# Rows split into half-precision parts and transposed by DMA, and half-precision pairs for queries and keys

## Chip, cores and metric

The kernel runs on one core of one Trainium2 chip. The metric is the device time of one execution in microseconds; the median of three runs is given. All times below come from the runs, from one profiled execution or from its trace.

## The reference

One layer of a hybrid encoder on 2048 rows of width 1024, all in float32:

- `h = rmsnorm(x)`, then one projection `h @ w_in` gives the queries, keys and values of 4 stick-breaking heads and of 8 chunked heads, and three 256-wide inputs of a gated convolution of width 3.
- Stick-breaking heads: `A[t,s] = sigmoid(z_ts) * prod over s<j<t of (1 - sigmoid(z_tj))`, with `z = q.k / 8` and `s < t`; the output is `A @ v`.
- Chunked heads: queries and keys are RMS-normalised per head (width 64), each chunk of 64 rows attends to itself and the 8 chunks before it, with a relative-position bias and a softmax.
- All outputs are RMS-normalised per head (`y`), then `x = x + y @ w_out`.
- `x = x + (silu(g @ w_gate) * (g @ w_up)) @ w_down`, with `g = rmsnorm(x)`; the inner width is 2816.

## The kernel before

Products run on TensorE as three matmuls of half-precision pairs: a float32 operand is split into a high part and the rest, and high x high, high x low and low x high are added in PSUM (`mm3`, lines 315 to 321). Both operands need the contracted dimension on the partitions, so every 128 normalised rows have to be transposed first.

The 2048 rows are cut in two halves of two groups of 512 rows. `hh` and `hl` are the transposed high and low parts of a group; there is one buffer of each for either group of a half, and the x rows, the y rows (normalised outputs of the heads) and the rows of the feed-forward all use them in turn. A class `Rows` (lines 341 to 371) makes them two blocks of 128 rows at a time: `ahead` calls `make` (load and normalise, `rms_rows`) and `to_T`, `need` makes sure that a pair is there, and `beside` spreads the next pair over the matmuls of the present one. `to_T` (lines 265 to 277) transposes 8 times on TensorE into a PSUM buffer of the tag `sc`, which the scores use too; ScalarE then copies the high part out and VectorE subtracts it to make the low part.

The program has four parts. `weave` interleaves by hand two generators: `fill` makes projections, convolutions, the normalisation of y and the first half's output projection, and `attend` gives pieces of attention. A clock of written-out costs (the numbers that the generators yield) says when the next piece of attention is taken; TensorE keeps this order. Attention pieces run in three steps, with a lag of 3 and 5 pieces between them: scores and weights (`front`), transposes of the weights (`mid`), product with V (`back`). Then come `ffn(0)`, the output projection of the second half (`out_proj`), and `ffn(1)`. The other engines' order is made by a scheduler. All transfers are issued by SyncE's queue (SP), in order: weights, rows, Q, K and V, stores of attention outputs and of intermediate results in DRAM. GpSimd subtracts for the low parts of weights (line 225) and adds the two halves of each finished attention tile (`put_y`, line 574).

Queries and keys go to DRAM (`kd`, `qd`) as high and low parts in F32R, written by `put_parts` (lines 423 to 431), and come back in `attend`: K holds the high part on 64 partitions and the low part on the other 64, and two query tiles hold the two orders, so that two matmuls give all products (`scores`, lines 577 to 587). For a piece of one key block (n = 1) `scores` also computes the 128 columns ahead of it. `y_norm` (lines 706 to 720) normalises y and stores it to `ynd`, from which `y_rows` loads it.

Of the kernel before, what the change touches and what calls it, by code (L numbers as in the profile page):

```python
# [22 lines left out]
NEG = -1e30  # L23
WSC = float(2 ** 14)
# [15 lines left out]
def trunk(ctx: ExitStack, tc: tile.TileContext, x, anw, w_in, qnw, knw, biasx, conv_w, onw, w_out,  # L40
# [18 lines left out]
    xp = ctx.enter_context(tc.tile_pool(name="xp", bufs=6))  # L59
# [12 lines left out]
    nc.gpsimd.affine_select(out=never, in_=never, pattern=[[1, 128]], compare_op=ALU.is_gt, fill=NEG,  # L72
# [4 lines left out]
    cw = consts.tile([128, 2, 3], F32, name="cw")  # L77
    halo = consts.tile([128, 2, 2], F32, name="halo")
# [4 lines left out]
    ynd = [dp.tile([128, D], F32, name=f"ynd{t}") for t in range(NB)]  # L83
# [181 lines left out]
    def to_T(xn, hh, hl, t):  # L265

        cs = slice(t * 128, (t + 1) * 128)
        for i in range(2):
            p = sc1()
            ks = slice(4 * i, 4 * i + 4)  # L270
            for k in range(4):
                c = (4 * i + k) * 128
                nc.tensor.transpose(p[:, k * 128:(k + 1) * 128], xn[:, c:c + 128], ident)  # L273
            pk = p.rearrange("p (k c) -> p k c", k=4)
            nc.scalar.copy(hh[:, ks, cs], pk)
            nc.vector.tensor_tensor(hl[:, ks, cs], pk, hh[:, ks, cs], ALU.subtract)
            yield 0.45
# [46 lines left out]
    kd, qd = [{(p, i, j): dp.tile([128, HT], F32R, name=f"{n}d{p}_{i}{j}")  # L324
# [8 lines left out]
    def late_consts():  # L333
        for i, w in enumerate((qnw, knw)):
            for s in range(2):
                nc.sync.dma_start(nw[s * 64:(s + 1) * 64, i:i + 1], w.rearrange("(p o) -> p o", o=1))
        nc.vector.tensor_scalar(nw[:, 0:1], nw[:, 0:1], HD ** -0.5, None, op0=ALU.mult)
        for b in range(2):
            nc.sync.dma_start(cw[:, b, :], conv_w[:, b * 128:(b + 1) * 128].rearrange("t p -> p t"))
# [115 lines left out]
    def stick_qk(H, groups, W, pair):  # L455
        key = ("qk", pair)
        u = W.get(key)
        for i, d in enumerate((kd, qd)):
            yield from proj_T(H, groups, u[i], lambda g, o, i=i, d=d: put_parts(o, pair, g, d, descale(key, i)))
# [117 lines left out]
    def scores(Q, cols, K, k0, n, diagonal=False):  # L577
# [3 lines left out]
        lead = 128 if n == 128 else 0  # L581
        kc = K[:, k0 - lead:k0 + n]
        nc.tensor.matmul(z[:, :n + lead], q1[:, cols], kc, start=True, stop=False)  # L583
        if diagonal:
            nc.tensor.matmul(z[:, lead:lead + 128], identb, never, start=False, stop=False)
        nc.tensor.matmul(z[:, :n + lead], q2[:, cols], kc, start=False, stop=True)
        return z[:, lead:lead + n]
# [4 lines left out]
    def stick_tile(T, head, K, k0, Q, V, cols):  # L592
# [3 lines left out]
        def piece(b, n):  # L596
# [3 lines left out]
            def front():  # L600
# [4 lines left out]
                nc.scalar.activation(be[:, :N], z, AF.Sigmoid, scale=HD ** -0.5)  # L605
                nc.scalar.activation(re[:, :N], z, AF.Sigmoid, scale=-HD ** -0.5)  # L606
# [28 lines left out]
    def chunk_tile(T, head, K, k0, Q, V, cols, bias):  # L635
# [4 lines left out]
        def front():  # L640
# [9 lines left out]
            nc.vector.tensor_scalar(nm, m[:, 0:1], other, -1.0, op0=ALU.max, op1=ALU.mult)  # L650
            tot = small(1, "tot")
            nc.scalar.activation(s[:, :n * 128], s[:, :n * 128], AF.Exp, bias=nm, accum_out=tot)
# [15 lines left out]
    def attend(half, groups, head):  # L668
# [4 lines left out]
        K = ap.tile([128, HT + more], F32R, name="k", tag="k")  # L673
        V = ap.tile([128, (HT + more) // 128, 2, HD], F16, name="v", tag="v")
        rows = slice(head % 2 * 64, head % 2 * 64 + 64)
        for j in range(2):
            at = slice(j * 64, j * 64 + 64)
            nc.sync.dma_start(f32(K[at, :HT]), f32(kd[head // 2, half, j][rows, :]))
            if more:
                nc.sync.dma_start(f32(K[at, HT:]), f32(kd[head // 2, 0, j][rows, :more]))  # L680
# [3 lines left out]
        if not stick:  # L684
            bias = ap.tile([128, CW], F32, name="bias", tag="bias")
            nc.sync.dma_start(bias, biasx[head - 4])
            nc.gpsimd.memset(bias[0:64, 576:640], NEG)
            nc.gpsimd.memset(bias[64:128, 0:64], NEG)
        for g in groups:
            c = where(g)[1]  # L690
            q1 = ap.tile([128, GRP], F32R, name="q1", tag="q")
            q2 = ap.tile([128, GRP], F32R, name="q2", tag="q")
            for j in range(2):
                src = f32(qd[head // 2, half, j][rows, c:c + GRP])
                for i, q in enumerate((q1, q2)):
                    at = (i + j) % 2 * 64
                    nc.sync.dma_start(f32(q[at:at + 64, :]), src)
# [8 lines left out]
    def y_norm(T, gain, tmp):  # L706
# [13 lines left out]
        nc.sync.dma_start(ynd[T], yt)  # L720
# [30 lines left out]
    def ffn_rows(H, groups):  # L751
        gain = []

        def make(g, b):
# [4 lines left out]
            return rms_rows(xt, gain[0])  # L759
# [260 lines left out]
```

## Time and profile before

| what | value |
|---|---|
| runs | 2720.06 us median of 3 (2718.31 to 2722.84) |
| profiled execution | 2721.8 us |
| its span, first to last instruction | 2719.9 us |
| granted TensorE clock, mean | 0.978 |
| TensorE busy | 2548.8 us (94%) |
| VectorE, ScalarE, GpSimd busy | 1472.0, 1046.1, 358.3 us |
| moved by DMA | 327.82 MB, 120 GB/s of HBM traffic over the span |

The span is what the trace shows; the time of the execution has some 2 us around it. Busy shares are means over stages of different kinds, so the windows by stage have to be read with them: the interleaved part lasts to about 1190 us, `ffn(0)` to 1910, the second output projection to 2036, and `ffn(1)` to the end. A granted clock of 1 is 2.4 GHz, 0.5 is 1.2 GHz.

### The profile page before, as it was taken

What the parts mean: (1) busy time and instruction counts of PE and PEld (TensorE: products, weight loads), DVE (VectorE), ACT (ScalarE), POOL (GpSimd) and SP (SyncE); (2) the same over time, 40 slices, a digit from 0 to 9 for tenths busy, and PEclk for the clock granted to TensorE, in tenths of its full rate; (3) what the DMA queues carried; (4) which work ended last, traced back from release to release, by engine and by line L of the source; (5) the groups of instructions that cost most, each with busy time, mean ns of one, the idle gap of its engine ahead of it and who ended that gap; (6) DMA issues with size and microseconds to landing.
All of it is one profiled execution on the core that took longest, in us unless ns stands there. A gap on an engine that the chain in (4) does not pass through costs nothing.

```text
span 2719.9 us, 41796 instructions
## 1 busy us (share of the span) xinstructions
PE 2548.8 (94%) x16258; PEld 1719.7 (63%) x16258; DVE 1472.0 (54%) x3535; ACT 1046.1 (38%) x1994; POOL 358.3 (13%) x389
## 2 busy tenths in 40 slices
PE   5998979998799889879999999999999999999999
PEld 4477766766687578754555555556864555555556
DVE  6467777689999878853443444333352333322234
ACT  5565756555455677663333333321121111111110
POOL 1123331102212211021111111110000000000000
PEclk8999989999999999989999999999999999999999
DMA  7644546554332267664332223232661111111101
GB/s 246 192 139 131 164 140 201 171 167 134 128 120 72 88 177 200 200 223 141 101 101 93 93 93 101 78 101 104 229 210 47 47 47 47 59 58 47 47 24 62
DMA packets 245063, 327.82 MB, mean 121 GB/s; under 512 B 77184, under 2 KB 168320, under 8 KB 244864
## 3 DMA queue, kind: packets, MB, share of 16 engines
q1 hardware_dynamic: 244864, 325.14, 37.8%
q8 instruction: 128, 2.10, 0.3%
q14 instruction: 71, 0.58, 0.1%
HBM read 220.21 MB, written 104.86 MB: 120 GB/s over the span
## 4 chain that ended last, share of the span: by engine, by line
PE 38%; DMA 4%; issue 4%; DVE 2%; POOL 1%; ACT 1%; SPq 0%; POOLq 0%; DVEq 0%; ACTq 0%
PE acc L318 7%; PE acc L320 7%; PE acc L319 7%; PE sc L937 5%; PE sc L938 5%; PE sc L939 5%; POOL w L225 1%; DMA wr<-in_w_down 1%; DMA x1d<-xs 1%; DMA wr<-in_w_up 1%; PE sc L273 0%; DMA xf<-x1d 0%; DVE gl L923 0%; DVE x L941 0%; DVE wl L258 0%
## 5 line engine op out<-in xcount | busy, mean ns | idle before, releaser
L318 PE MATMUL acc<-hh,w 128*128 128x512 f16 x1728 | 657.5, 381 | 0.0
L319 PE MATMUL acc<-hl,w 128*128 128x512 f16 x1728 | 656.3, 380 | 0.0
L320 PE MATMUL acc<-hh,w 128*128 128x512 f16 x1728 | 656.1, 380 | 0.0
L919 DVE SCALAR_TENSOR_TENSOR sg<-acc,ds,sg 128x512 f32<-128x512 f32 x88 | 66.0, 750 | 615.3 <-PE acc L320 533.5
L318 PE MATMUL acc<-w,hh 128*128 128x256 f16 x1408 | 392.5, 279 | 5.5 <-ACT w L224 4.0
L319 PE MATMUL acc<-w,hh 128*128 128x256 f16 x1408 | 390.4, 277 | 1.8 <-POOL w L225 1.8
L320 PE MATMUL acc<-w,hl 128*128 128x256 f16 x1408 | 390.1, 277 | 1.3 <-DVE rry L102 1.3
L941 DVE TENSOR_TENSOR x<-sc,x 128x512 f32<-128x512 f32 x352 | 241.3, 690 | 200.5 <-PE sc L939 193.7
L320 PEld LDWEIGHTS <-w 128*128 128x128 f16 x1728 | 169.3, 98 | 204.9 <-issue 1.8
L318 PEld LDWEIGHTS <-w 128*128 128x128 f16 x1728 | 169.3, 98 | 192.3 <-issue 15.8
L937 PE MATMUL sc<-wh,gh 128*128 128x512 f32 x704 | 278.7, 396 | 4.5 <-DVE x L941 4.5
L319 PEld LDWEIGHTS <-w 128*128 128x128 f16 x1728 | 169.6, 98 | 175.1 <-issue 1.1
L939 PE MATMUL sc<-wh,gl 128*128 128x512 f32 x704 | 274.2, 390 | 0.0
L938 PE MATMUL sc<-wl,gh 128*128 128x512 f32 x704 | 274.2, 389 | 0.0
L225 POOL TENSOR_TENSOR w<-wr,w 128x1024 f16<-128x1024 f32 x76 | 163.4, 2170 | 579.1 <-ACT w L224 523.6
L551 DVE SCALAR_TENSOR_TENSOR wtl<-tp,wth 128x512 f16<-128x512 f32 (+3 forms) x384 | 200.0, 529 | 50.5 <-ACT wth L550 49.7
L609 DVE TENSOR_TENSOR_SCAN re<-re,zero 128x512 f32<-128x512 f32 (+3 forms) x160 | 185.8, 1161 | 48.6 <-ACT re L606 48.3
L550 ACT ACTIVATE wth<-tp 128x512 f16<-128x512 f32 (+3 forms) x384 | 175.5, 475 | 81.9 <-PE tp L548 79.0
L922 ACT CAST gh<-sg 128x512 fp32r<-128x512 f32 x88 | 54.3, 617 | 378.7 <-DVE sg L919 378.7
L583 PE MATMUL sc<-k,q 128*128 128x320 f32 (+3 forms) x384 | 161.8, 425 | 4.8 <-ACT re L606 1.8
L318 PEld LDWEIGHTS <-hh 128*128 128x128 f16 x1408 | 140.1, 100 | 41.1 <-issue 19.9
L223 ACT ACTIVATE wr<-wr,wsc 128x1024 f32<-128x1024 f32 x76 | 83.4, 1141 | 191.2 <-DVE wsc L214 191.1
(153 smaller groups left out, 3798.2 us busy)
## 6 DMA issues: line engine op xcount, KB each, us to landing
w<-wd SPq DMA_DIRECT2D x92, 512.0 KB, 4.2
wd<-w SPq DMA_DIRECT2D x76, 512.0 KB, 2.7
q<-qd SPq DMA_DIRECT2D x192, 128.0 KB, 2.9
wr<-in_w_down SPq DMA_DIRECT2D x44, 512.0 KB, 4.3
k<-kd SPq DMA_DIRECT2D x56, 256.0 KB, 4.0
wr<-in_w_gate SPq DMA_DIRECT2D x22, 512.0 KB, 4.8
wr<-in_w_up SPq DMA_DIRECT2D x22, 512.0 KB, 6.0
xt<-in_x SPq DMA_DIRECT2D x16, 512.0 KB, 5.6
```

Source lines behind the costliest of these rows:

```text
L225: nc.gpsimd.tensor_tensor(w[:, 1, :], raw, w[:, 0, :], ALU.subtract)
L318: nc.tensor.matmul(o, sh(k), mh(k), start=(k == 0), stop=False)
L319: nc.tensor.matmul(o, sh(k), ml(k), start=False, stop=False)
L320: nc.tensor.matmul(o, sl(k), mh(k), start=False, stop=(k == n - 1))
L550: nc.scalar.activation(wh[:, s], tp[:, c], AF.Copy, scale=WSC)
L551: nc.vector.scalar_tensor_tensor(wl[:, s], tp[:, c], WSC, wh[:, s], op0=ALU.mult, op1=ALU.subtract)
L583: nc.tensor.matmul(z[:, :n + lead], q1[:, cols], kc, start=True, stop=False)
L609: nc.vector.tensor_tensor_scan(re[:, :N], re[:, :N], zero.to_broadcast([128, N]), start, ALU.mult, ALU.add)
L937: nc.tensor.matmul(o, gh[:, cs], wh[:, cc], start=st, stop=False)
L938: nc.tensor.matmul(o, gh[:, cs], wl[:, cc], start=False, stop=False)
L939: nc.tensor.matmul(o, gl[:, cs], wh[:, cc], start=False, stop=en)
L941: nc.vector.tensor_tensor(x1, o, x1, ALU.add)
```

## The change

Three things change. First, `split_rows` makes a high and a low half-precision part of the normalised rows while these still lie along the free dimension (ScalarE casts, GpSimd subtracts), and `to_T` becomes two DMA transposes of 128x1024 half-precision elements, issued on SyncE's queue. The y rows are split in `y_norm` before they are stored, and transposed straight from DRAM. The cost that `to_T` yields to the clock falls from 2 x 0.45 to 2 x 0.1 for a block. Second, queries and keys become F16 pairs with power-of-two scales, which are taken out again where scores are read; the bias is scaled on GpSimd to match. Third, `scores` loses the extra 128 columns of single blocks.

```diff
-    xp = ctx.enter_context(tc.tile_pool(name="xp", bufs=6))
+    xp = ctx.enter_context(tc.tile_pool(name="xp", bufs=5))
...
-    ynd = [dp.tile([128, D], F32, name=f"ynd{t}") for t in range(NB)]
+    ynd = [dp.tile([128, 2, D], F16, name=f"ynd{t}") for t in range(NB)]
...
-    def to_T(xn, hh, hl, t):
+    def split_rows(xn):
+
+        x16 = xp.tile([128, 2, D], F16, name="x16", tag="x16", bufs=2)
+        nc.scalar.copy(x16[:, 0, :], xn)
+        nc.gpsimd.tensor_tensor(x16[:, 1, :], xn, x16[:, 0, :], ALU.subtract)
+        return x16
+
+    def to_T(x16, hh, hl, t):
 
         cs = slice(t * 128, (t + 1) * 128)
-        for i in range(2):
-            p = sc1()
-            ks = slice(4 * i, 4 * i + 4)
-            for k in range(4):
-                c = (4 * i + k) * 128
-                nc.tensor.transpose(p[:, k * 128:(k + 1) * 128], xn[:, c:c + 128], ident)
-            pk = p.rearrange("p (k c) -> p k c", k=4)
-            nc.scalar.copy(hh[:, ks, cs], pk)
-            nc.vector.tensor_tensor(hl[:, ks, cs], pk, hh[:, ks, cs], ALU.subtract)
-            yield 0.45
+        for j, h in enumerate((hh, hl)):
+            nc.sync.dma_start_transpose(h[:, :, cs], x16[:, j, :])
+            yield 0.1
...
-    kd, qd = [{(p, i, j): dp.tile([128, HT], F32R, name=f"{n}d{p}_{i}{j}")
+    ZS = {}
+    kd, qd = [{(p, i, j): dp.tile([128, HT], F16, name=f"{n}d{p}_{i}{j}")
...
-            return rms_rows(xt, gain[0])
+            return split_rows(rms_rows(xt, gain[0]))
...
     def y_rows(H, groups):
         def make(g, b):
-            yt = xp.tile([128, D], F32, name="yt", tag="xt")
-            nc.sync.dma_start(yt, ynd[g * 4 + b])
-            return yt
+            return ynd[g * 4 + b]
...
-        hi = ap.tile([128, 520], F32R, name="sth", tag="w2")[:, :GRP]
-        lo = ap.tile([128, 520], F32R, name="stl", tag="w2")[:, :GRP]
-        nc.scalar.activation(hi, src, AF.Copy, scale=scale)
-        nc.vector.scalar_tensor_tensor(lo, src, scale, f32(hi), op0=ALU.mult, op1=ALU.subtract)
-        for part, st in enumerate((hi, lo)):
-            nc.sync.dma_start(f32(d[pair, half, part][:, c:c + GRP]), f32(st))
+        st = ap.tile([128, 2, 520], F16, name="st", tag="w2")[:, :, :GRP]
+        nc.scalar.activation(st[:, 0, :], src, AF.Copy, scale=scale)
+        nc.vector.scalar_tensor_tensor(st[:, 1, :], src, scale, st[:, 0, :], op0=ALU.mult, op1=ALU.subtract)
+        for part in range(2):
+            nc.sync.dma_start(d[pair, half, part][:, c:c + GRP], st[:, part, :])
...
-        lead = 128 if n == 128 else 0
-        kc = K[:, k0 - lead:k0 + n]
-        nc.tensor.matmul(z[:, :n + lead], q1[:, cols], kc, start=True, stop=False)
+        kc = K[:, k0:k0 + n]
+        nc.tensor.matmul(z[:, :n], q1[:, cols], kc, start=True, stop=False)
...
-                nc.scalar.activation(be[:, :N], z, AF.Sigmoid, scale=HD ** -0.5)
-                nc.scalar.activation(re[:, :N], z, AF.Sigmoid, scale=-HD ** -0.5)
+                nc.scalar.activation(be[:, :N], z, AF.Sigmoid, scale=ZS[head // 2][:, 0:1])
+                nc.scalar.activation(re[:, :N], z, AF.Sigmoid, scale=ZS[head // 2][:, 1:2])
...
-            nc.scalar.activation(s[:, :n * 128], s[:, :n * 128], AF.Exp, bias=nm, accum_out=tot)
+            nc.scalar.activation(s[:, :n * 128], s[:, :n * 128], AF.Exp, bias=nm, scale=qks[:, 1:2],
+                                 accum_out=tot)
...
-        K = ap.tile([128, HT + more], F32R, name="k", tag="k")
+        K = ap.tile([128, HT + more], F16, name="k", tag="k")
...
             nc.sync.dma_start(bias, biasx[head - 4])
+            nc.gpsimd.tensor_scalar(bias, bias, qks[:, 0:1], None, op0=ALU.mult)
...
-            q1 = ap.tile([128, GRP], F32R, name="q1", tag="q")
-            q2 = ap.tile([128, GRP], F32R, name="q2", tag="q")
+            q1 = ap.tile([128, GRP], F16, name="q1", tag="q")
+            q2 = ap.tile([128, GRP], F16, name="q2", tag="q")
...
-        nc.sync.dma_start(ynd[T], yt)
+        nc.sync.dma_start(ynd[T], split_rows(yt))
```

Left out are the constants of the scales: `qks` (the power-of-two scale of normalised queries times keys, its inverse and its negative, from the two gains), made once in `late_consts` by some ten small VectorE instructions, and `ZS` (two per pair of stick-breaking heads). The fill value for masked scores becomes -1e37.

## Rows read from the trace of the kernel before

**Rows 1.** The page: span, and busy time of each engine.
```profile
span 2719.9 us, 41796 instructions
PE 2548.8 (94%) x16258; PEld 1719.7 (63%) x16258; DVE 1472.0 (54%) x3535; ACT 1046.1 (38%) x1994; POOL 358.3 (13%) x389
```

**Rows 2.** Windows by stage: length, busy us of each engine, clock, DMA share, GB/s.
```profile
408.00:545.00 137.00, 132.05 (x1067) 96.76 (x1066) 95.83 (x357) 83.44 (x214) 14.34 (x47) 1.00 0.63 185
545.00:885.00 340.00, 306.95 (x2693) 236.94 (x2692) 314.31 (x652) 188.28 (x382) 73.62 (x74) 0.98 0.40 125
885.00:1190.00 305.00, 271.68 (x2557) 226.87 (x2556) 238.56 (x784) 208.81 (x469) 53.51 (x97) 0.96 0.55 162
1190.00:1221.00 31.00, 16.98 (x76) 10.39 (x75) 20.71 (x64) 23.40 (x36) 9.01 (x4) 0.71 0.89 306
1221.00:1910.00 689.00, 684.45 (x3113) 396.76 (x3112) 265.75 (x504) 195.76 (x267) 95.36 (x44) 1.00 0.31 103
1910.00:2036.00 126.00, 118.36 (x973) 98.14 (x972) 58.04 (x139) 28.45 (x51) 0.00 (x0) 0.97 0.67 227
```

**Rows 3.** The same windows for line 273 (transposes) alone: TensorE, weight loads.
```profile
408.00:545.00 137.00, 9.51 (x64) 7.26 (x64) 1.00 0.63 185
885.00:1190.00 305.00, 16.56 (x96) 12.59 (x96) 0.96 0.55 162
1910.00:2036.00 126.00, 19.77 (x128) 16.03 (x127) 0.97 0.67 227
```

**Rows 4.** The chain in order of time, second output projection: start, us, what.
```profile
1913.76 0.44 PE sc L273 x4
```

**Rows 5.** Waits of TensorE, 67 to 1190 us: total, times, longest.
```profile
PE tp L548 <- DVE wtl L551: 43.6, 32, 4.6
PE sc L273 <- DVE xf L312: 5.4, 2, 3.7
```

**Rows 6.** Groups by line and form: busy us, mean ns, idle before.
```profile
L276 DVE TENSOR_TENSOR hl<-sc,hh 128x512 f16<-128x512 f32 x96 | 64.3, 685 | 19.7 <-ACT hh L275 19.4
L275 ACT CAST hh<-sc 128x512 f16<-128x512 f32 x96 | 54.8, 588 | 84.9 <-PE sc L273 84.8
L225 POOL TENSOR_TENSOR w<-wr,w 128x1024 f16<-128x1024 f32 x76 | 163.4, 2170 | 579.1 <-ACT w L224 523.6 <-issue 29.2 <-DMA xt<-in_x 18.4
L224 ACT CAST w<-wr 128x1024 f16<-128x1024 f32 x76 | 75.4, 1036 | 0.1
L586 PEld LDWEIGHTS sc<-k,q 128*128 128x128 f32 x384 | 75.5, 197 | 3.7 <-issue 2.4
L318 PEld LDWEIGHTS <-hh 128*128 128x128 f16 x1408 | 140.1, 100 | 41.1 <-issue 19.9 <-ACT hh L275 1.7
```

**Rows 7.** Waits of SyncE's queue, whole span.
```profile
SPq L575 <- POOL yu L574: 297.5, 151, 15.3
```

**Rows 8.** DMA: the queue's packets, MB, share; issues with KB, median us to landing.
```profile
q1 hardware_dynamic: 244864, 325.14, 37.8%
v<-vd SPq DMA_DIRECT2D x28, 256.0 KB, 3.5
ydr<-yu SPq DMA_DIRECT2D x192, 32.0 KB, 2.3
```

**Rows 9.** Timeline of the lead-in: first transposes and last low half.
```profile
11.96 1.94 PE L273 MATMUL sc<-ident,xt 128*128 128x128 f32 x8 [11.96 <-DVE xt L312]
63.88 0.68 DVE L276 TENSOR_TENSOR hl<-sc,hh 128x512 f16<-128x512 f32 x1
```

**Rows 10.** Timeline of VectorE before the first feed-forward.
```profile
1204.93 1.28 DVE L312 SCALAR_TENSOR_TENSOR xf<-xf,rry,gain 128x1024 f32<-128x1024 f32 x1
1216.96 1.28 DVE L312 SCALAR_TENSOR_TENSOR xf<-xf,rry,gain 128x1024 f32<-128x1024 f32 x1
1220.98 0.69 DVE L276 TENSOR_TENSOR hl<-sc,hh 128x512 f16<-128x512 f32 x1 [0.16 <-ACT hh L275]
```

**Rows 11.** Timeline of SyncE's queue at the end of the first feed-forward.
```profile
1892.22 16.32 SPq L980 DMA_DIRECT2D out<-x  x7
```

More of the change, by code (lines that the diff above doesn't have):

```diff
@@ L23 @@
 NEG = -1e30
+NEVER = -1e37
 WSC = float(2 ** 14)
@@ L77, in trunk @@
     cw = consts.tile([128, 2, 3], F32, name="cw")
+    qks = consts.tile([128, 3], F32, name="qks")
     halo = consts.tile([128, 2, 2], F32, name="halo")
@@ L337, in late_consts @@
         nc.vector.tensor_scalar(nw[:, 0:1], nw[:, 0:1], HD ** -0.5, None, op0=ALU.mult)
+        row = small(128, "nwr")
+        m = small(2, "nwm")
+        for i, w in enumerate((qnw, knw)):
+            nc.sync.dma_start(row[:, 64 * i:64 * i + 64],
+                              bass.AP(tensor=w.tensor, offset=w.offset, ap=[[0, 128], [1, HD]]))
+        nc.vector.tensor_reduce(m, row.rearrange("p (n d) -> p n d", d=HD), axis=AX.X, op=ALU.max,
+                                apply_absolute_value=True)
+        nc.vector.tensor_scalar(m[:, 0:1], m[:, 0:1], HD ** -0.5, None, op0=ALU.mult)
+        nc.vector.tensor_scalar(m, m, 1e-12, None, op0=ALU.max)
+        t = m.bitcast(I32)
+        nc.vector.tensor_scalar(t, t, 23, None, op0=ALU.logical_shift_right)
+        nc.vector.tensor_scalar(t, t, -1.0, float(2 * 127 + 9), op0=ALU.mult, op1=ALU.add)
+        nc.vector.tensor_scalar(t, t, 23, None, op0=ALU.logical_shift_left)
+        nc.vector.tensor_tensor(nw, nw, m, ALU.mult)
+        nc.vector.tensor_tensor(qks[:, 0:1], m[:, 0:1], m[:, 1:2], ALU.mult)
+        nc.vector.reciprocal(qks[:, 1:2], qks[:, 0:1])
+        nc.vector.tensor_scalar(qks[:, 2:3], qks[:, 1:2], -1.0, None, op0=ALU.mult)
         for b in range(2):
@@ L457, in stick_qk @@
         u = W.get(key)
+        if pair not in ZS:
+            zs = consts.tile([128, 2], F32, name=f"zs{pair}")
+            nc.vector.tensor_tensor(zs[:, 0:1], descale(key, 0), descale(key, 1), ALU.mult)
+            nc.vector.tensor_scalar(zs[:, 0:1], zs[:, 0:1], HD ** -0.5 / DOWN ** 2, 1e-30, op0=ALU.mult,
+                                    op1=ALU.max)
+            nc.vector.tensor_scalar(zs[:, 1:2], zs[:, 0:1], -1.0, None, op0=ALU.mult)
+            ZS[pair] = zs
         for i, d in enumerate((kd, qd)):
-            yield from proj_T(H, groups, u[i], lambda g, o, i=i, d=d: put_parts(o, pair, g, d, descale(key, i)))
+            yield from proj_T(H, groups, u[i], lambda g, o, i=i, d=d: put_parts(o, pair, g, d, DOWN))
     def chunk_qk(H, groups, W, pair):
@@ L580, in scores @@
         z = sc1()
-        lead = 128 if n == 128 else 0
-        kc = K[:, k0 - lead:k0 + n]
-        nc.tensor.matmul(z[:, :n + lead], q1[:, cols], kc, start=True, stop=False)
+        kc = K[:, k0:k0 + n]
+        nc.tensor.matmul(z[:, :n], q1[:, cols], kc, start=True, stop=False)
         if diagonal:
-            nc.tensor.matmul(z[:, lead:lead + 128], identb, never, start=False, stop=False)
-        nc.tensor.matmul(z[:, :n + lead], q2[:, cols], kc, start=False, stop=True)
-        return z[:, lead:lead + n]
+            nc.tensor.matmul(z[:, :128], identb, never, start=False, stop=False)
+        nc.tensor.matmul(z[:, :n], q2[:, cols], kc, start=False, stop=True)
+        return z[:, :n]
     def open_av():
@@ L677, in attend @@
             at = slice(j * 64, j * 64 + 64)
-            nc.sync.dma_start(f32(K[at, :HT]), f32(kd[head // 2, half, j][rows, :]))
+            nc.sync.dma_start(K[at, :HT], kd[head // 2, half, j][rows, :])
             if more:
-                nc.sync.dma_start(f32(K[at, HT:]), f32(kd[head // 2, 0, j][rows, :more]))
+                nc.sync.dma_start(K[at, HT:], kd[head // 2, 0, j][rows, :more])
         nc.sync.dma_start(V[:, :HT // 128], vd[head // 4 * 4, half][:, :, head % 4])
@@ L690, in attend @@
             c = where(g)[1]
[L691 to L692 removed]
+            q1 = ap.tile([128, GRP], F16, name="q1", tag="q")
+            q2 = ap.tile([128, GRP], F16, name="q2", tag="q")
             for j in range(2):
[L694 removed]
+                src = qd[head // 2, half, j][rows, c:c + GRP]
                 for i, q in enumerate((q1, q2)):
                     at = (i + j) % 2 * 64
[L697 removed]
+                    nc.sync.dma_start(q[at:at + 64, :], src)
             for t in range(3, -1, -1):
@@ L758, in make @@
                 gain.append(gain_row("f"))
-            return rms_rows(xt, gain[0])
+            return split_rows(rms_rows(xt, gain[0]))
         return Rows(H, groups, make)
```

4 lines of the change are left out of this document (2 added, 2 removed).

## The prediction

> **What bounds the kernel now.** I read the page's busy shares first: TensorE (PE) 94%, VectorE (DVE) 54%, ScalarE (ACT) 38%, GpSimd (POOL) 13% [rows 1]. So TensorE is the bound on average, and the next question is where it is not. The windows by stage answer that [rows 2]. From 1221 to 1910 us (the first half's feed-forward) TensorE is busy for 684 of 689 us. In the interleaved part before it, three stages differ: 408 to 545 us is TensorE's (132 of 137 us); 545 to 885 us is DVE's (314 of 340 us, TensorE 307); 885 to 1190 us is shared (272 of 305 us, DVE 239). From 1190 to 1221 us TensorE works 17 of 31 us at a granted clock of 0.71, a mix of the full 2.4 GHz and 1.2 GHz: it waits for rows there. So work taken off TensorE is paid in full in some stages, in part in others, and not at all where a chain of small steps sets the pace. The windows of line 273 alone give the place of the transposes: 64 from 408 to 545 us, 96 from 885 to 1190, 128 from 1910 to 2036 [rows 3]; the other 96 of the 384 are 64 in the lead-in and 32 from 1190 to 1221.
>
> **The transposes leave TensorE.** Four of them are 0.44 us of the chain [rows 4], 110 ns each; all 384 are 42 us. In 408 to 545 us, 64 x 0.11 = 7.0 us at full worth. In 885 to 1190, 96 x 0.11 = 10.6 us, taken at TensorE's share of that stage (0.89): 9.4 us. In 1910 to 2036, the 64 of the y rows and the first 32 of the feed-forward's, 10.6 us. The lead-in and the 64 in front of the two feed-forwards lie in chains of waits; there I count the latency instead, below. TensorE's in-order waits in front of them go too: 5.4 us for the normalised row alone between 67 and 1190 us [rows 5]; with those for free score buffers I take 6 us. What takes their place is a matmul's wait for landed columns, hidden while the rows are made a pair ahead.
>
> **Scores.** A 128x128 weight load of F32R takes 197 ns, one of F16 100 ns [rows 6]. It overlaps the matmul before it, so the gain lies between nothing and 97 ns for each of 384 pairs (37 us). TensorE's loads keep pace with its matmuls in most groups, so I take about a fifth, 8 us, the narrow groups' dropped 128 leading columns included.
>
> **VectorE and ScalarE.** 96 subtractions of 685 ns (64 us) leave DVE; 96 copies of 588 ns become 48 casts of about 1036 ns on ACT, a wash [rows 6]. None of the subtractions lies in DVE's own stage, 545 to 885 us. In 885 to 1190 us 24 x 0.685 = 16 us leave an engine busy for 239 of 305 us; DVE's late halves of a transposed tile make TensorE wait 43.6 us there and before [rows 5], so something comes of it: 2 us, bounds 0 and 10. Writing Q and K parts in F16 trims 96 instructions a little, on engines that have slack outside 545 to 885 us: I count nothing.
>
> **POOL and the queue of SyncE (SP).** POOL gets 48 subtractions of about 2.17 us [rows 6] and 16 scalings of the bias. It is 13% busy, but it is in order, and the small additions of each finished attention tile stand behind them; behind those additions stand ACT's next copy of a tile (two buffers) and SP's stores, which already wait 297.5 us in all for them [rows 7]. Bounds: nothing (the wait falls into slack) and 44 x 0.6 us = 26 us; I take 8 us lost (28 subtractions and 16 scalings inside the interleaved part, about 0.2 us each). SP gets 96 transposes and loses 16 loads of y rows. A transpose of x or feed-forward rows waits on SP for POOL, and K, Q and weight loads stand behind it; they are issued a head or a group ahead, so I add nothing to the 8 us.
>
> **The price of one DMA transpose** is the unknown, 128x1024 F16, 256 KB each. No row shows one. Below: from 1190 to 1221 us the engines move 306 GB/s at a share of 0.89 [rows 2], 344 GB/s when full, so 256 KB takes 0.76 us of all of them, and a 256 KB load whose runs are also 256 bytes lands 3.5 us after its issue [rows 8]. Middle: each run of 128 columns is 256 bytes, so 1024 runs; a packet takes 0.378 x 16 x 2719.9 / 244864 = 67 ns on average [rows 8], and 1024 / 16 of them 4.3 us. Above: eight 32 KB transfers in series at 2.3 us [rows 8], 18.4 us. It is one issue of a plain size with long runs, so I take the geometric middle of 0.76 and 4.3, 2 us from one transpose to the next, and 4 us to land.
>
> The Trainium skill has a rule against this change: its page "VectorE: DVE Perf Modes", section "The three transpose paths", gives 390 ns for a 128x128 transpose on TensorE and 1309 ns through the DMA crossbar, and advises TensorE where PSUM will do. By that, 8 x 1.3 = 10.5 us each (an estimate), and the sum below would end some hundreds of us slower. Its page "Advanced Engine Details and Errata", section "X-Bar Transpose (TRN2)", says such DMAs are as fast as ordinary ones, which is my lower end. No row here decides between the two.
>
> **What the pitch costs in the three exposed places.** Lead-in: from the first transpose to the last low half 52.6 us pass for 16 halves of rows [rows 9], 3.3 us each, so a pitch of 2 is hidden; I take 3 us for the longer first latency. Before each feed-forward: the last low half now follows the last normalised row by 3.4 us (1218.24 to 1221.67) [rows 10]; afterwards by 1.04 (cast) + 2.17 (subtraction) + 4 = 7.2 us, so 3.8 us are lost, twice, 7.6 us. With pitch p the eight transposes there end 1.04 + 8p + 2 us after the first row (1206.2) against 15.5 us now: above p = 2 that is the larger loss. Before the second half's output projection the y transposes start as soon as the last gate product has read the columns; SP waits 16.3 us there for the last down-projections [rows 11], which covers eight at p = 2.
>
> **Sum.** Gains 7.0 + 9.4 + 10.6 + 6 + 8 + 2 = 43 us; losses 8 + 3 + 7.6 = 19 us. Net 24 us off the profiled execution's 2721.8 us: 2697.8 us; that execution is 1.7 us above the median of the runs, so 2697 us.
>
> **Rivals.** (1) *Slower: transposes set the pace.* If a transpose follows the one before by p, the losses are 16(p - 3.3) in the lead-in, twice 8p + 3 - 15.5 before the feed-forwards, and 8p - 21.3 before the output projection (16 us of cover and 5.3 us of the first pair's matmuls), each where positive. They eat the gains of 35 us (43 less POOL's 8) at p = 3.3; at the mean packet's 4.3 they are 16 + 44 + 13 = 73 us, and the time is 2760 us; at 5 us 2788. For it: nearly all packets are priced near 67 ns; against it: plain 256 KB transfers are far below. 0.31. (2) *The stages are not TensorE's.* If 885 to 1190 us is set by the chain through DVE (its wait is the longest there [rows 5]), the 9.4, 6, 2 and most of the score term vanish: 19 us of gain against 19 us of loss, 2720 us. 0.14. (3) *The change does more:* all 42 us, 20 us of loads, no loss at POOL, and the row waits of 1190 to 1221 us moved under attention tiles, since the shorter written-out cost of a row lets the output projection end earlier: 2655 us or below, 0.05, part of the faster side.
>
> **Numbers.** Forecast and its spread between 2655 and 2714: 0.50; below 0.05; same 0.14; slower 0.31, of which 0.20 up to 2790. The likeliest case's own range is 2655 to 2714. The range 2655 to 2790 leaves out 0.05 below and 0.11 above. This kernel can be told from no change at about 0.2%, 5.4 us. Faster 0.55, same 0.14, slower 0.31.
>
> **What would show it.** The landing and pitch of the transposes in the list of DMA issues (4 and 2 us); line 273 gone from TensorE; 408 to 545 us shorter by about 7 us; 1910 to 2036 us by about 7; the gap before the first gate product longer by 3 to 4 us. Wrong if the pitch is above 3.3 us, if SP's waits for POOL grow and the attention tiles stall with them, or if the stage of 885 to 1190 us keeps its length.

## The result, and the profile after

The changed kernel takes 2784.06 us (median of 4 runs, 2780.36 to 2787.29), the kernel before 2719.88 us on the same chip: a ratio of 1.0234, 95% interval 1.0216 to 1.0252. It is slower by 64 us. The profiled execution took 2787.3 us.

The top of the page of the changed kernel answers to [rows 1]:

```profile
span 2784.9 us, 41067 instructions
PE 2530.3 (91%) x15874; PEld 1657.7 (60%) x15874; DVE 1445.1 (52%) x3455; ACT 1077.5 (39%) x1946; POOL 502.1 (18%) x453
```

The 384 transposes have left TensorE, but its busy time fell by 18.5 us, not 42; 11 us of the difference are slower matmuls of the down-projections, shown below. POOL grew by 144 us. The windows by stage, cut where the same attention tiles, residual rows and products of the feed-forward are reached as in [rows 2]:

```profile
432.00:575.00 143.00, 127.58 (x997) 85.40 (x995) 86.19 (x318) 81.80 (x196) 35.14 (x59) 0.98 0.62 157
575.00:930.00 355.00, 311.28 (x2696) 236.48 (x2695) 324.06 (x658) 209.18 (x389) 102.41 (x82) 0.95 0.27 84
930.00:1236.00 306.00, 254.49 (x2424) 200.80 (x2423) 221.51 (x762) 213.34 (x453) 74.65 (x106) 0.96 0.60 164
1236.00:1272.00 36.00, 7.39 (x27) 2.94 (x27) 21.46 (x51) 16.78 (x24) 16.07 (x8) 0.60 0.75 231
1272.00:1962.00 690.00, 686.83 (x3100) 395.09 (x3099) 265.90 (x501) 204.54 (x275) 112.61 (x52) 1.00 0.33 103
1962.00:2090.00 128.00, 107.89 (x856) 86.01 (x854) 45.09 (x110) 19.02 (x27) 17.01 (x8) 0.93 0.80 235
```

No stage became shorter. The first lasts 143 us instead of 137, with 4.5 us less work on TensorE: the engine idles 15 us where it idled 5. VectorE's stage is 355 instead of 340 us, and VectorE is busy for 324 instead of 314. Ahead of the feed-forward TensorE works 7 of 36 us, at a mean granted clock of 0.60, a mix of 1.2 and 2.4 GHz.

The new transfers, from the list of DMA issues (times each, median us to landing), answer to [rows 8]:

```profile
hh<-x SPq DMA_TRANSPOSE x32, 3.1
hl<-x SPq DMA_TRANSPOSE x32, 2.8
hh<-ynd SPq DMA_TRANSPOSE x16, 4.4
hl<-ynd SPq DMA_TRANSPOSE x16, 4.1
```

The transposes are cheap. By line, one holds SP for 1.25 to 1.31 us (median by kind), and it lands about as fast as the plain loads of `v` (3.4 us here). Sixteen of them in a row, ahead of the second output projection, keep SP from 1910.3 to 1933.9 us, 1.5 us each. The waits of TensorE between 67 and 1280 us answer to [rows 5]:

```profile
PE tp L572 <- DVE wtl L575: 64.6, 50, 6.2
PE acc L320 <- DMA hh<-x: 26.1, 2, 25.2
PE av L585 <- ACT yu L597: 15.9, 14, 2.7
PE tp L572 <- DVE be L637: 11.0, 6, 4.1
```

The wait for VectorE's late halves grew by 21 us, and one wait of 25.2 us for landed columns is new. SP's waits for finished tiles, which I had expected to grow, answer to [rows 7] and fell from 297.5 us:

```profile
SPq L599 <- POOL yu L598: 251.7, 110, 9.4
```

The wait for landed columns is the gap before the feed-forward. The timeline of ScalarE there shows that the columns are late because the casts are:

```profile
1250.87 1.05 ACT L270 CAST x<-xf 128x1024 f16<-128x1024 f32 x1
1257.57 1.05 ACT L270 CAST x<-xf 128x1024 f16<-128x1024 f32 x1 [3.66 <-DVE xf L314]
1261.98 1.05 ACT L270 CAST x<-xf 128x1024 f16<-128x1024 f32 x1 [1.23 <-DVE xf L314]
1267.56 1.05 ACT L270 CAST x<-xf 128x1024 f16<-128x1024 f32 x1 [4.54 <-DVE xf L314]
```

and the casts wait for VectorE, whose timeline has

```profile
1252.06 2.07 DVE L115 SCALAR_TENSOR_TENSOR rrt<-rrt,rry 128x1 f32<-128x1 f32 x1
1254.24 1.97 DVE L116 TENSOR_TENSOR rry<-rry,rrt 128x1 f32<-128x1 f32 x1
...
1258.71 3.18 DVE L314 SCALAR_TENSOR_TENSOR xf<-xf,rry,gain 128x1024 f32<-128x1024 f32 x1
```

Line 115 works on one column and takes 0.16 us elsewhere in this stretch; line 314 takes 1.28 us otherwise. POOL's timeline says what goes on beside them:

```profile
1251.99 2.13 POOL L271 TENSOR_TENSOR x<-xf,x 128x1024 f16<-128x1024 f32 x1 [13.52 <-ACT x L270]
1254.08 2.12 POOL L227 TENSOR_TENSOR w<-wr,w 128x1024 f16<-128x1024 f32 x1
1258.69 2.13 POOL L271 TENSOR_TENSOR x<-xf,x 128x1024 f16<-128x1024 f32 x1 [2.49 <-ACT x L270]
```

The first two slow instructions of VectorE begin just after one of POOL and end with it (1254.13 and 1254.12, 1256.21 and 1256.20); the third begins 0.02 us after POOL's of 1258.69, and from that one's end it still takes 1.07 us. From this came the theories.

### The profile page after: what moved, and what is told of

Its sections match the earlier page's. It is cut to its first block, busy times and chain, and to the rows that moved or that the text cites. A ratio compares the mean times of both kernels' runs of the same rounds, so it can differ in the third digit from the quotient of the medians.

```text
span 2784.9 us, 41067 instructions
## 1 busy us (share of the span) xinstructions
PE 2530.3 (91%) x15874; PEld 1657.7 (60%) x15874; DVE 1445.1 (52%) x3455; ACT 1077.5 (39%) x1946; POOL 502.1 (18%) x453
## 5 line engine op out<-in xcount | busy, mean ns | idle before, releaser
L320 PE MATMUL acc<-w,hh 128*128 128x256 f16 x1408 | 400.4, 284 | 22.8 <-DMA hh<-x 13.5
L322 PE MATMUL acc<-w,hl 128*128 128x256 f16 x1408 | 399.3, 284 | 4.3 <-DMA hl<-x 4.2
L321 PE MATMUL acc<-w,hh 128*128 128x256 f16 x1408 | 399.9, 284 | 1.8 <-POOL w L227 1.8
L632 DVE TENSOR_TENSOR_SCAN re<-re,zero 128x512 f32<-128x512 f32 (+3 forms) x160 | 192.3, 1202 | 53.5 <-ACT re L629 53.0
L320 PEld LDWEIGHTS <-hh 128*128 128x128 f16 x1408 | 144.1, 102 | 43.6 <-DMA hh<-x 19.9
L598 POOL TENSOR_TENSOR yu<-yu 128x64 f32<-128x64 f32 x192 | 78.1, 408 | 501.4 <-ACT yu L597 485.2
L321 PEld LDWEIGHTS <-hh 128*128 128x128 f16 x1408 | 143.6, 102 | 36.6 <-issue 8.5
```

The costliest lines, as they stand in the source:

```text
L320: nc.tensor.matmul(o, sh(k), mh(k), start=(k == 0), stop=False)
L321: nc.tensor.matmul(o, sh(k), ml(k), start=False, stop=False)
L322: nc.tensor.matmul(o, sl(k), mh(k), start=False, stop=(k == n - 1))
L598: nc.gpsimd.tensor_tensor(u[:, :HD], u[:, :HD], u[:, HD:], ALU.add)
L632: nc.vector.tensor_tensor_scan(re[:, :N], re[:, :N], zero.to_broadcast([128, N]), start, ALU.mult, ALU.add)
```

## The experiments

Theory *POOL*: a subtraction of rows on GpSimd holds up VectorE while it runs, and finished tiles behind it; this costs most where VectorE sets the pace. Rivals: *order* (the smaller written-out cost of a row shifts the attention pieces against the projections), *F16* (queries and keys), *queue* (SP's queue behind transposes) and *chain* (the longer way from a normalised row to landed columns, where nothing covers it). The median of the kernel before lay between 2717.9 and 2720.3 us in all comparisons. A ratio compares runs of one chip; two rows of the table can come from different chips, so differences of a few us between rows are near the noise.

| run | us | ratio to before, 95% |
|---|---|---|
| e1_cost | 2778.26 | 1.0220 (1.0203 to 1.0237) |
| e2_qk16 | 2723.49 | 1.0020 (1.0009 to 1.0031) |
| e3_rows | 2763.85 | 1.0168 (1.0148 to 1.0188) |
| e4_dve | 2760.86 | 1.0156 (1.0137 to 1.0174) |
| e5_pad | 2786.43 | 1.0243 (1.0221 to 1.0264) |
| e6_yonly | 2741.55 | 1.0082 (1.0064 to 1.0101) |
| e7_xf | 2778.10 | 1.0216 (1.0193 to 1.0239) |
| e8_yu4 | 2754.77 | 1.0129 (1.0114 to 1.0144) |
| e9_qk16_pad | 2714.72 | 0.9979 (0.9966 to 0.9992) |
| e10_cost_pad | 2739.06 | 1.0069 (1.0050 to 1.0088) |
| e11_pool | 2736.07 | 1.0062 (1.0041 to 1.0083) |
| e12_queue | 2786.11 | 1.0243 (1.0223 to 1.0263) |
| e13_ffpe | 2717.64 | 0.9996 (0.9984 to 1.0009) |
| e14_ylate | 2712.95 | 0.9978 (0.9967 to 0.9988) |
| e15_after_pad | 2769.62 | 1.0185 (1.0167 to 1.0203) |
| e16_yu4 | 2710.33 | 0.9960 (0.9946 to 0.9975) |
| e17_best | 2704.36 | 0.9949 (0.9934 to 0.9963) |
| e18_gain | 2706.30 | 0.9956 (0.9943 to 0.9969) |

**Which part of the change.** e2_qk16 is the kernel before with the edits of queries, keys, bias and `scores`; e3_rows is the kernel before with `split_rows`, the DMA transposes and their buffers.

> The kernel before with only the second and third part of the change: queries and keys as F16 pairs with power-of-two scales, the bias scaled on GpSimd, no extra columns for single blocks; rows are transposed on TensorE as before. Theory POOL, and theory order too: the F16 parts save loads and matmul columns, the 16 scalings on GpSimd cost a little: 2705 to 2720 us. Rival theory (the F16 queries and keys carry the loss, through the scalings and the narrower steps): 2735 to 2765 us.

> The kernel before with only the first part of the change: rows split by ScalarE and GpSimd and transposed by DMA, with the new written-out cost 0.1 and the smaller buffer pool; queries and keys stay F32R pairs. If the rows carry the loss (theory POOL or theory order): 2775 to 2800 us. If the F16 queries and keys carry it: 2715 to 2740 us.

The rows carry it: 45 us alone, the F16 part 4 us. Both times lie outside the ranges of either theory. Together the parts cost 64, so some 15 us are more than the sum; what makes them was not tried. The F16 part is no gain either, which I had not expected; e9_qk16_pad comes back to it.

**Subtraction and written-out cost.** In the changed kernel,

```diff
 e1_cost:  to_T
-            yield 0.1
+            yield 0.45
 e4_dve:   split_rows
-        nc.gpsimd.tensor_tensor(x16[:, 1, :], xn, x16[:, 0, :], ALU.subtract)
+        nc.vector.tensor_tensor(x16[:, 1, :], xn, x16[:, 0, :], ALU.subtract)
```

> The changed kernel with one number changed: a transposed half block again yields 0.45 to the written-out clock instead of 0.1. Nothing else differs, so no engine does more or less work. Theory order (the smaller number lets the projections run ahead of the attention pieces, whose last steps then stand bare): the 46 us that arise in the interleaved part shrink by at least 20, 2740 to 2765 us. Theory POOL (GpSimd's added subtractions and scalings hold up VectorE and the stores): the number does not matter, 2775 to 2795 us.

> The changed kernel with the 48 subtractions of the rows' low parts on VectorE instead of GpSimd. Theory POOL: 28 of them no longer hold up the tile additions and VectorE's port in the interleaved part, and the gaps before the two feed-forwards shrink by some 10 us: 2745 to 2765 us. Theory order: only the gaps before the feed-forwards shrink, 2770 to 2785 us.

Moving 48 subtractions from an engine that is 18% busy to one that is 52% busy gains 23 us. By the starts of POOL's additions of finished tiles in the two traces, 20 us of it arise before the 97th tile (604.9 against 585.2 us), where the x rows are made, and 5 us from there to the 121st. The cost alone gains 6 us by the medians; the intervals of the two versions overlap, so that is not settled.

**The suspected cost by itself.** In the kernel before, in `y_norm`:

```diff
         nc.gpsimd.tensor_tensor(yt, yt, gain, ALU.mult)
+        spare = xp.tile([128, D], F16, name="spare", tag="spare", bufs=2)
+        nc.gpsimd.tensor_tensor(spare, yt, gain, ALU.subtract)
```

> The kernel before with one more GpSimd instruction in every y_norm: a subtraction of 128x1024 into a spare tile that nobody reads, right behind the multiplication with the gain. No other instruction, no wait and no transfer hangs on it. Theory POOL (while GpSimd runs an instruction of two inputs VectorE's small ones are held, and tiles wait behind it): the eight in VectorE's stage cost 1 to 2.5 us each, 8 to 20 us, 2728 to 2740 us. Rival (GpSimd's own time is slack, and the loss of the rows comes from the longer chain of cast, subtraction and transfer): 2718 to 2724 us.

16 us, for 16 instructions that nobody waits for. (The traced execution is the shortest of the four, 10 us above that of the kernel before.) VectorE's stage, from the 97th to the 121st finished attention tile, first in the kernel before (window as in [rows 2]; groups by line and form):

```profile
576.00:882.00 306.00, 273.05 (x2451) 216.15 (x2449) 290.13 (x600) 167.00 (x336) 70.29 (x67) 0.98 0.36 114
...
L609 DVE TENSOR_TENSOR_SCAN re<-re,zero 128x512 f32<-128x512 f32 x66 | 85.1, 1289 | 7.3 <-ACT re L606 7.3
L614 DVE TENSOR_TENSOR be<-be,re 128x511 f32<-128x511 f32 x67 | 54.8, 818 | 0.3
L551 DVE SCALAR_TENSOR_TENSOR wtl<-tp,wth 128x512 f16<-128x512 f32 x67 | 45.1, 674 | 0.0
L612 DVE TENSOR_TENSOR be<-be,re 128x1 f32<-128x1 f32 x60 | 14.1, 234 | 1.9 <-ACT be L605 1.7
...
L714 DVE TENSOR_REDUCE ya<-ysq 128x8 f32<-128x512 f32 x16 | 10.5, 673 | 0.0
```

and in e11_pool:

```profile
572.00:893.00 321.00, 281.00 (x2453) 221.28 (x2451) 305.01 (x601) 167.04 (x336) 93.66 (x75) 0.95 0.34 109
...
L609 DVE TENSOR_TENSOR_SCAN re<-re,zero 128x512 f32<-128x512 f32 x67 | 87.9, 1312 | 8.9 <-ACT re L606 8.8
L614 DVE TENSOR_TENSOR be<-be,re 128x511 f32<-128x511 f32 x67 | 58.2, 869 | 0.3
L551 DVE SCALAR_TENSOR_TENSOR wtl<-tp,wth 128x512 f16<-128x512 f32 x67 | 45.1, 674 | 0.0
L612 DVE TENSOR_TENSOR be<-be,re 128x1 f32<-128x1 f32 x60 | 15.9, 266 | 1.9 <-ACT be L605 1.7
...
L714 DVE TENSOR_REDUCE ya<-ysq 128x8 f32<-128x512 f32 x16 | 10.5, 673 | 0.0
```

The stage is 15 us longer, and VectorE, with the same work (600 and 601 instructions), is busy for 14.9 us more: 8 spare subtractions at 1.9 us each. The other eight lie in the first feed-forward, where TensorE sets the pace, and cost nothing: from the first down-projection on, the traced executions take 1431.1 and 1432.2 us. What grew are mostly instructions with two inputs in SBUF (lines 609, 612, 614 and the small ones of the norms), 13 of the 15 us. Line 551, which reads one of its inputs from PSUM, and line 714, which reads one tile, kept their time to the nanosecond. The Trainium skill has this rule on its page "SBUF — State Buffer", section "Who interferes with whom": a VectorE instruction with two SBUF inputs and a GpSimd instruction that reads SBUF use the same port, whichever starts first has it for its whole length, and an instruction with at most one SBUF input is not concerned, outside the 2-port modes that the page names. The rows agree: the first two held instructions ahead of the feed-forward end with POOL's to 0.01 us, and lines 551 and 714 kept their 674 and 673 ns. It is the rule to have looked up.

**y rows against the others.** In the changed kernel the PE version of `to_T` is put back for some rows: e6_yonly leaves DMA transposes (and the split) to y rows only, e7_xf to x and feed-forward rows only.

> The changed kernel, but only the y rows are split and transposed by DMA; the x rows and those of the feed-forwards are transposed on TensorE with the old written-out cost. Theory POOL (the loss arises where VectorE sets the pace, 545 to 885 us, where the eight y_norms of the first half put a cast and a subtraction each): about half of the rows' loss of 45 us is here, 2740 to 2755 us. Rival (the loss comes from the rows that lie in chains of waits, x in the lead-in and those before the feed-forwards): 2720 to 2732 us.

> The counterpart: only the x rows and those of the feed-forwards are split and transposed by DMA; the y rows are stored in F32 and transposed on TensorE. Theory POOL: the gaps before the two feed-forwards and the lead-in carry 20 to 35 us, 2742 to 2758 us. Rival (the chains of waits carry nearly all): 2765 to 2785 us.

Against e2_qk16 (ratio 1.0020), y rows alone cost 0.62% or 17 us, the x and feed-forward rows alone 1.96% or 53 us; both theories had a part, and mine gave too little to the chains. By the finished tiles, the stretch from the 97th to the 121st lasts 320 us in e6_yonly and 307 in e7_xf, against 301 in e2_qk16; the 97th itself starts at 573, 599 and 572 us. So the y rows lose in VectorE's stage, and the x rows ahead of it. The two runs' losses overlap: together the rows cost 58 us.

**SP's queue and the buffers of finished tiles.** Both start from e4_dve; e12_queue has the four buffers too.

```diff
 e8_yu4:
-  ... vst=1, yu=2, bias=2)
+  ... vst=1, yu=4, bias=2)
 e12_queue:  to_T
-            nc.sync.dma_start_transpose(h[:, :, cs], x16[:, j, :])
+            nc.scalar.dma_start_transpose(h[:, :, cs], x16[:, j, :])
```

> The kernel with the rows' subtraction on VectorE (2761 us), with four buffers instead of two for the finished attention tiles on their way from ScalarE over GpSimd to the store. Theory queue (the stores of finished tiles stand in SP's queue behind transposes, and TensorE's product with V then waits for ScalarE's copy): the waits of the av accumulator, 17.5 us there, go, and the time falls by 8 to 17 us, 2744 to 2753 us. Rival (these waits only move to the next wait in the stage, which VectorE or the lag between the pieces sets): 2757 to 2764 us.

> The kernel with the subtraction on VectorE and four buffers for finished tiles (2755 us), with the transposes issued on ScalarE's queue instead of SP's. Theory queue (each transpose holds SP for about 1.25 us and waits there for free columns, with the loads and stores behind it): the time falls by 5 to 15 us, 2740 to 2750 us. Rival (SP has time; on ScalarE the same issues stand in front of the copies and exponentials): 2758 to 2785 us.

Four buffers gain 6 us, which lies between the two ranges; TensorE's waits of the av accumulator, which theory queue wanted gone, only fell from 17.5 to 14.5 us. ScalarE as the queue loses 31: TensorE then waits 66.9 us for `hh<-x`, and ScalarE's copies now stand behind its issues. So SP is the better place; whether a free queue would gain was not tried. Later the same buffers were put into a version without any DMA transpose:

> The kernel with F16 queries and keys and the unused buffer (2715 us), rows transposed on TensorE, with four buffers instead of two for the finished attention tiles. If two buffers are short only because transposes stand in SP's queue: no change, 2711 to 2718 us. If they were short before too (the waits of the av accumulator were 9.6 us in the kernel before): 2703 to 2710 us.

2710.33 against 2714.72 us, intervals that just overlap. The same edit from e14_ylate to e17_best, below, gains 0.29% (0.9978 to 0.9949) with intervals apart, and there no transpose by DMA runs beside the attention. So the two buffers were short without the transposes too, and these 4 to 6 us are probably not the change's fault.

**The feed-forward's matmuls.** In all versions with F16 queries and keys and without the unused buffer tried below, the F32R matmuls of the down-projection, which no line of the diff touches, are slower. Page of the kernel before, then of the changed one (mean ns behind the comma):

```profile
L939 PE MATMUL sc<-wh,gl 128*128 128x512 f32 x704 | 274.2, 390 | 0.0
L938 PE MATMUL sc<-wl,gh 128*128 128x512 f32 x704 | 274.2, 389 | 0.0
```

```profile
L963 PE MATMUL sc<-wl,gh 128*128 128x512 f32 x704 | 277.9, 395 | 0.0
L964 PE MATMUL sc<-wh,gl 128*128 128x512 f32 x704 | 277.9, 395 | 0.0
```

The added small tiles of `late_consts` (four buffers of 512 and of 32 bytes) lie between the weights' buffers and those of the feed-forward, and move the latter by 2176 = 2048 + 128 bytes against the former; the added constants move everything.

```diff
 e5_pad (all buffers 32 bytes further):
+    pad = consts.tile([128, 8], F32, name="pad")
 e9_qk16_pad, e15_after_pad (1920 = 2048 - 128 bytes between the two):
+    pad = xp.tile([128, 480], F32, name="pad", tag="pad", bufs=1)
```

> The changed kernel with one unused constant of 32 bytes per partition, so that every later buffer begins 32 bytes further on. In the runs with F16 queries and keys, whose added constants move these buffers, a matmul of the down-projections takes 395 to 400 ns, in the kernel before and in the one with the rows alone 389 to 395 ns. Theory place (where the buffers of the down-projection lie makes the difference): 389 ns again, 2112 matmuls x 5.5 ns = 12 us less, 2770 to 2776 us. Rival (something else in the F16 part does it): 395 ns stays, 2780 to 2790 us.

> F16 queries and keys with the rows transposed on TensorE as before (2723 us), and one unused buffer of 1920 bytes per partition ahead of the feed-forward's buffers, so that these stand to the weights' buffers at the same distance modulo 2048 bytes as in the kernel before (128 bytes off in all runs with F16 queries and keys). Theory distance: the down-projections' matmuls go back from 395 to 400 ns to 389, 12 us less, 2709 to 2714 us, faster than both kernels. Rival (the distance does not matter): 395 ns stays, 2718 to 2726 us.

> The changed kernel with the unused buffer of 1920 bytes and nothing else. Theory distance: 2112 matmuls take 389 ns instead of 395 to 400, 12 us less: 2769 to 2776 us. Rival (the gain came from something else in that version): 2780 to 2790 us.

Moving everything by 32 bytes changes nothing, and my first idea fell. The second holds: the changed kernel gains 14 us from an unused buffer, 11 us of them in the three lines of the down-projections, and the page of e15_after_pad has

```profile
L966 PE MATMUL sc<-wh,gl 128*128 128x512 f32 x704 | 274.2, 390 | 0.0
L965 PE MATMUL sc<-wl,gh 128*128 128x512 f32 x704 | 274.2, 389 | 0.0
```

All eight runs that have this buffer show 389 to 390 ns on these lines, all nine other runs with F16 queries and keys 395. Whether the distance counts or the place of the feed-forward's buffers alone is not separated: e5_pad moved them by 32 bytes only. With the unused buffer F16 queries and keys alone are 0.2% faster than the kernel before (e9_qk16_pad), 9 us better than e2_qk16.

**What is left.** e10_cost_pad is e8_yu4 with cost 0.45 and the 1920 bytes; e13_ffpe is that with the feed-forwards' rows transposed on TensorE again.

> The rows by DMA at their best so far: the kernel with the subtraction on VectorE and four buffers for finished tiles (2755 us), with the old written-out cost of 0.45 and the unused buffer of 1920 bytes. Theory distance takes 12 us, theory order some 6: 2734 to 2742 us. If neither holds for this version: 2750 to 2758 us. On every theory it stays slower than before, since VectorE's stage still has the rows' subtractions.

> The best version of the rows by DMA so far (2739 us; subtraction on VectorE, four tile buffers, old written-out cost, unused buffer of 1920 bytes), with the rows of the two feed-forwards transposed on TensorE. Theory chain (nearly all that is left lies in the rows right before the feed-forwards, where the longer way from a normalised row to landed columns is bare): 2713 to 2722 us. Rival (what is left lies in the interleaved part): 2728 to 2738 us.

The waits of TensorE from 1190 to 1290 us in e10_cost_pad, and from 1150 to 1300 us in e13_ffpe:

```profile
PE acc L322 <- DMA hh<-x: 25.3, 1, 25.3
```

```profile
PE sc L291 <- DVE xf L330: 11.5, 4, 5.3
```

The gap of 25 us stays even without POOL's subtractions, and goes with the feed-forwards' DMA transposes: 21 us, theory chain. In the traces the stretch from the 121st finished tile to the first down-projection becomes 12 us shorter, and that between the two halves' down-projections 13. The casts in e10_cost_pad, on ScalarE's timeline, show why:

```profile
1214.57 1.03 ACT L272 CAST x<-xf 128x1024 f16<-128x1024 f32 x1
1219.81 1.04 ACT L272 CAST x<-xf 128x1024 f16<-128x1024 f32 x1 [1.04 <-DVE xf L316]
1223.99 1.04 ACT L272 CAST x<-xf 128x1024 f16<-128x1024 f32 x1 [3.14 <-DVE xf L316]
1228.44 1.04 ACT L272 CAST x<-xf 128x1024 f16<-128x1024 f32 x1 [3.41 <-DMA hl<-x]
```

They wait for VectorE's rows, and the fourth for the landing of an earlier row, since `x16` has two buffers. The first product of the second group comes 25.0 us after the first row's square (1209.46 to 1234.48), in e9_qk16_pad, with TensorE's transposes, 19.9 (1196.58 to 1216.50). The square itself comes 21 us after the last store of `x1d` (1188.2) instead of 15 (1181.4), behind weights for which ScalarE waits. That is 11 us of one gap; the second feed-forward's I did not take apart.

**Versions beyond both.** e14_ylate is e9_qk16_pad with DMA transposes for the y rows of the second half only, split on VectorE during `ffn(0)`; e17_best adds the four buffers; e18_gain is e17_best with the gain of `y_norm` multiplied on VectorE.

> The kernel with F16 queries and keys and the unused buffer (2715 us), in which the y rows of the second half alone are split (on VectorE, during the first feed-forward) and transposed by DMA ahead of the second output projection. Theory: TensorE sets the pace there and the eight rows' transposes are 64 x 0.11 = 7 us of it: 2706 to 2712 us. Rival (the time of the output projection is set by the rows' chain into the second feed-forward): 2713 to 2717 us.

> F16 queries and keys, unused buffer, late y rows by DMA (2713 us) with four buffers for the finished tiles (worth 4 us without the late y rows): 2706 to 2711 us if the two add up; 2711 to 2714 us if not.

> The same with the multiplication by the gain in y_norm on VectorE instead of GpSimd; eight of the 16 lie in the stage where VectorE sets the pace. Theory POOL: each holds VectorE there for about what the spare subtraction cost (1.9 us), and costs 1.2 us on VectorE itself, so 8 x 0.7 = 5 us are gained: 2701 to 2706 us. Rival (an engine that sets the pace should be spared every instruction): 8 x 1.2 = 10 us lost, 2714 to 2720 us.

e14_ylate alone can't be told from e9_qk16_pad (2712.95 against 2714.72). e17_best is 0.5% faster than the kernel before, the fastest of all runs, and faster than either of its ranges. e18_gain met neither theory: in VectorE's stage, 572 to 875 us, the eight multiplications add 11.3 us to VectorE, and its busy time is 283.1 against 285.7 us. They cost 1.4 us each and release 1.7, and the stage from the 97th to the 121st tile keeps its length (302.7 and 302.3 us).

## Why the prediction was wrong, step by step

The runs make a staircase from the changed kernel to the one before, each step one edit or two:

| from, to | edit | us |
|---|---|---|
| after, e4_dve | rows' subtraction off POOL | -23.2 |
| e4_dve, e8_yu4 | four tile buffers | -6.1 |
| e8_yu4, e10_cost_pad | distance (14.4 by e15_after_pad) and cost | -15.7 |
| e10_cost_pad, e13_ffpe | feed-forwards' rows on TensorE | -21.4 |
| e13_ffpe, e16_yu4 | x and y rows on TensorE, six `xp` buffers | -7.3 |
| e16_yu4, e9_qk16_pad | two tile buffers | +4.4 |
| e9_qk16_pad, before | F32R queries and keys, no pad | +5.2 |

The traces say where the steps lie. Stretches in us, between the starts of POOL's additions of finished tiles and the matmuls of the down-projections; each column is one profiled execution:

| stretch | before | after | e4_dve | e13_ffpe | e16_yu4 |
|---|---|---|---|---|---|
| start to 97th tile | 575.8 | 604.9 | 585.2 | 579.0 | 573.7 |
| 97th to 121st tile | 305.4 | 321.2 | 316.0 | 314.9 | 302.5 |
| 121st tile to first down-projection | 407.6 | 416.0 | 411.2 | 395.6 | 399.5 |
| down-projections, first half | 620.8 | 622.9 | 625.2 | 623.0 | 620.7 |
| from there to the second half's | 192.6 | 196.1 | 197.2 | 183.6 | 192.9 |
| down-projections, second half | 612.6 | 618.9 | 618.8 | 612.6 | 612.6 |

VectorE's stage in e13_ffpe, whose y rows are split there, and in e16_yu4 (as in [rows 2]):

```profile
579.00:894.00 315.00, 275.67 (x2450) 216.88 (x2449) 293.65 (x606) 186.26 (x343) 74.69 (x63) 0.95 0.24 77
573.70:876.20 302.50, 268.72 (x2450) 212.34 (x2449) 285.31 (x598) 178.65 (x334) 73.19 (x62) 0.97 0.28 90
```

- **POOL, "I take 8 us lost".** This step failed. Its upper bound, 26 us, holds the measured 23, but by luck: I priced finished tiles that queue behind POOL, and SP's waits for them fell. What the runs show instead is VectorE held while POOL works: 1.9 us for each spare subtraction in VectorE's stage (e11_pool). That the same explains the 20 us before the 97th tile is not shown by a run of its own; there the subtraction also stands in the rows' chain, with 2.13 us on POOL against 1.22 on VectorE.
- **545 to 885 us, priced at nothing.** I left this stage out because no subtraction of `to_T` lay there; the eight new casts and subtractions of `y_norm` do. The stage lost 16 us in the changed kernel, and 12 us still with the subtractions on VectorE (e13_ffpe against e16_yu4): 8 us more of busy time there, the rest idle.
- **VectorE's late halves, 2 us gained.** TensorE's waits for them grew from 43.6 to 64.6 us instead.
- **Before the feed-forwards, "3.8 us lost, twice".** Mis-sized: 21 us for both. I counted the way of the last row alone, 7.2 us in place of 3.4, and let nothing but the transposes' pitch lengthen the steps between rows. But cast, subtraction, VectorE's next row and two buffers wait for each other, so the whole way from the first row became 5 us longer, and it began 6 us later (e10_cost_pad against e9_qk16_pad).
- **408 to 545 us, 7.0 us at full worth.** This gain did not arrive. The stage lost TensorE work and became 6 us longer: once work left it, it was no longer TensorE's. Up to the 97th tile e13_ffpe, with x rows by DMA, is 5 us behind e16_yu4.
- **885 to 1190 us, 9.4 us and 6 us of waits.** In the changed kernel the stage kept its length (306 us), the sign that I had named. Without POOL's subtractions a part arrives: from the 121st tile to the first down-projection e13_ffpe is 4 us ahead of e16_yu4.
- **Second output projection, 10.6 us.** The gain for the y rows, 7 of the 10.6, is there where the feed-forwards' rows stay on TensorE: between the two halves' down-projections e13_ffpe is 9 us ahead of e16_yu4, while e14_ylate is only 2.5 us ahead of e9_qk16_pad. In the changed kernel the chain of the feed-forward's rows, just behind, takes more than that.
- **Scores, 8 us.** About right: 5 us (e9_qk16_pad), once the distance is restored.
- **Price of a transpose, 2 us pitch, 4 us landing.** Right: 1.25 us on SP, 1.5 us in a row of sixteen, 2.8 to 4.4 us to land. The cheap end of the two rules that I weighed holds: what the Trainium skill's page "VectorE: DVE Perf Modes" gives per 128x128 block in "The three transpose paths", 1309 ns, is about what eight such blocks take of the queue here.
- **Lead-in, 3 us.** The first finished tile is copied at 122.0 us instead of 118.6, as forecast, but by luck: in e4_dve, with the same transfers and the subtractions on VectorE, it is copied at 116.5. The longer latency that I priced did not show.
- **Rival 1** gives 2788 us at a pitch of 5 us. The time came out near it, but the pitch was at most 1.5 us, so its cause did not occur. The 14 us of the buffers' distance stood in no term and no rival. (The sum itself ends 1 us off: 2697.8 less 1.7 is 2696.)

So the 7 us by which e13_ffpe is slower than e16_yu4 are a sum of large parts: 12 us lost in VectorE's stage and 5 ahead of it, and some 13 us won in two stretches where TensorE's work shrinks. e17_best, which keeps the late y rows alone, has 302.7 us in VectorE's stage and 186.4 between the two halves' down-projections.

Still open: what share the written-out cost has (1 to 6 us), how much of the 20 us before the 97th tile is VectorE being held, and what makes the two parts of the change cost 15 us more together than alone. Rows by DMA with POOL's other work in VectorE's stage moved away were not tried.

## What to carry to other kernels

Ask of each instruction added on GpSimd not how busy GpSimd is, but what VectorE does at that moment: with two SBUF inputs on both sides, most of its length was added to VectorE's here. Time freed on the busiest engine is paid only up to the next limit of the stage, so price it by what bounds the stage when that work is gone. When time changes in a stage that the diff does not touch, look whether a buffer moved.

## What the hardware showed that I had not expected

- Beside POOL instructions of 2.1 us, one-column VectorE instructions took up to 2.07 us instead of 0.16; a spare instruction cost VectorE 1.9 us in e11_pool.
- F32R matmuls of 128x512 take 395 instead of 389 to 390 ns when the buffers of the two operands stand 128 bytes further apart modulo 2048, and the time comes back at 2048; the F16 ones of the same shape did not change (379 ns in the second feed-forward of e2_qk16 and of the kernel before). Distances between these two were not tried, and the place of one buffer alone is not ruled out.
- Scales read from a tile instead of a constant cost time: over the whole span, ScalarE's exponential of 128x640 went from 827 to 920 ns, VectorE's `nm` from 210 to 269 ns; e2_qk16, with TensorE's transposes, has 921 and 269.
- A DMA transpose of 128x1024 half-precision elements takes about as long to land as a plain transfer of 256 KB, but holds the issuing queue for 1.25 us, where the plain 256 KB load of `v` holds it for 0.56 and that of a row tile (`xf<-x1d`, ahead of the first feed-forward) for 0.38.
